# A hybrid four-layer model in fp32 halves: ScalarE, VectorE, GpSimd and the DMA queue ordered by the compiler's other timing model

## The chip, the cores and the metric

The kernel runs on one core of a Trainium2 chip. The metric is the device time in microseconds (us) of one execution. Of the kernel before, three runs are given, with a median of 2611.88 us (2609.99 to 2614.97).

## What is computed

Four layers act on 1040 tokens (16 meta tokens ahead of 1024) of width 1024. Each normalises the running sum `h`, runs one mixer and adds its output to `h`:

```python
for i in range(DEPTH):            # DEPTH = 4; kinds 0, 1, 2, 0
    u = rmsnorm(h, norm_gain[i])
    if kind == 0:   y = attention_branch(u, ...)   # 16 heads, window 128, sinks
    elif kind == 1: y = mlstm_branch(u, ...)       # 8 heads, 128 x 256 state
    else:           y = hgrn2_branch(u, ...)       # 8 heads, 128 x 128 state
    h = h + y
# attention: s = q k^T / 8 in a band; p = exp(s - m) / (sum + exp(sink - m)); o = p v
```

The products are carried in fp32 as sums over a high and a low half of each operand.

## The kernel before

All matmuls work on three column chunks of the tokens (400, 384 and 256 wide). A projection (L254, L299) multiplies weight tiles `wh`, `wl` with the normalised input `uh`, `ul`: three matmuls for each product (high by high, high by low, low by high), eight 128-row pieces deep. The output projections (L337) do the same with `yh`, `yl` and are added to the row `x` by VectorE (L340).

A helper, `split`, makes the halves: a cast on ScalarE (`s.copy`, L187), then a subtraction on VectorE (L188). It serves the weights (128x512, two for each weight tile), the inputs and the outputs alike, so each weight tile costs ScalarE two casts.

The attention layers (the first and the last) run over eight tiles `t` of two heads each. For each group of query blocks and each of the two heads `hh`, a unit is a chain of engines. In `S_step` TensorE makes the scores `pm` (L614, L615), ScalarE copies them into `Sm` (L634), VectorE merges the band (L635) and takes the maximum (L636, L637), ScalarE takes the exponential with its sum (L639), VectorE the reciprocal (L641) and ScalarE scales the row (L643). In `T_step` TensorE then transposes `Sm` (L660) and VectorE masks the result into `Pt` (L663). In `V_step` TensorE multiplies `Pt` with the values (L682) and ScalarE copies the sum out (L685):

```python
for u in range(nu):                                   # end of S_step
    s.activation(Sm[:, u, :P], Sm[:, u, :P], AF.Identity, scale=den[:, u : u + 1])   # L643
...
for u in range(nu):                                   # T_step
    pe.transpose(pt[:, u, :], Sm[:, u, :P], ident)                                   # L660
```

Beside these chains run the projections of the next tile. Their results are handled by the same engines: ScalarE reads `pj` (L519, L520), makes the scales (L536, L538) and splits the queries (casts, L491); VectorE turns them by their positions (L550 to L552). DMAs (L523) rotate the halves of a head. Outer units with a sink use L624, L626 and L628.

The second layer (mLSTM) runs eight heads, 131.8 us apart, each with nine blocks in a chain of its own (L890 to L958) woven into the next head's projections. The third (HGRN2) makes for each region of two blocks the scaled rows `X` by levels (VectorE L1152, L1153, ScalarE L1154, VectorE L1155), multiplies them (L1178), and carries a state `S` (L1255).

What sets the order: the program lists steps with costs in TensorE time, woven by hand. TensorE keeps that order exactly (`tc.manual_schedule` for PE). The other engines are ordered by the compiler's scheduler: it keeps a timeline of its own, and an engine that is free there takes the ready instruction of the highest priority. Priority is the place in the program, and steps wrapped in `hi` (the mixers' chains) count as 40 places earlier. The result is one fixed queue for each engine. In the trace each of these queues is worked off in that order. How long an instruction takes in the scheduler's timeline comes from a timing model, and this is chosen where the context is opened.

## Time and profile before

| | |
|---|---|
| median of the three runs | 2611.88 us |
| the profiled execution's own time | 2610.83 us |
| its span, first to last instruction | 2609.0 us |
| TensorE (PE) busy | 2558.0 us, 98% |
| VectorE (DVE) busy | 1980.3 us, 76% |
| ScalarE (ACT) busy | 1725.9 us, 66% |
| GpSimd (POOL) busy | 154.1 us, 6% |
| mean granted TensorE clock | 0.995 |
| share of the last chain that is TensorE | 81% |

TensorE is the bound: it is idle for 51 us of the span in all, some 15 us of it in the first 60 us. The other engines have idle time, and what they do matters where TensorE waits for it. In the profile PEld is TensorE's weight load, which overlaps its matmuls. In the rows below, a name such as `pt<-ident,Sm` reads: `pt` is written, `ident` and `Sm` are read. A timeline row gives the start, the duration, the engine, the line and the operation, and in brackets how long the engine was idle before it, and who ended that. A waits row gives the total in us, the number of waits and the longest.

### The profile page before, as it was taken

The numbers are of one execution on the slowest core, as the hardware profiler recorded it, in microseconds if no ns is written. First come the engines' busy times: TensorE is split into PE (matmuls) and PEld (weight loads), VectorE is DVE, ScalarE is ACT, GpSimd is POOL, SyncE is SP. The second block draws the span as 40 slices with busy tenths as digits, with TensorE's granted clock in tenths as the row PEclk, the third lists the DMA queues.
The fourth block names the chain that finished last, engine by engine and source line by source line (L and its number), as shares of the span: only waits on it lengthen the run. The fifth ranks groups of instructions, "written<-read, shape, count | busy, mean of one in ns | idle before, by whom it ended". The sixth has DMA issues, their size and how long they took to land.

```text
span 2609.0 us, 56062 instructions
## 1 busy us (share of the span) xinstructions
PE 2558.0 (98%) x21048; PEld 2459.0 (94%) x21048; DVE 1980.3 (76%) x5487; ACT 1725.9 (66%) x4757; POOL 154.1 (6%) x538
## 2 busy tenths in 40 slices
PE   7999999999999999999999999999999999999999
PEld 6899889899999999999999999999999999999999
DVE  6677777986767676767677788978787978677776
ACT  6777776566464646464646857878585867768872
POOL 1100100000000000000000000201001011000000
PEclk9999999999999999999999999999999999999999
DMA  4111111021111111111110101011110111111112
GB/s 136 56 43 50 46 37 47 17 67 58 41 58 41 58 41 58 41 58 41 55 61 34 57 27 42 30 38 34 34 42 26 42 62 45 54 44 47 53 38 82
DMA packets 74048, 126.81 MB, mean 49 GB/s; under 512 B 11552, under 2 KB 25760, under 8 KB 73776
## 3 DMA queue, kind: packets, MB, share of 16 engines
q1 hardware_dynamic: 73776, 123.23, 14.5%
q8 instruction: 165, 2.70, 0.4%
q14 instruction: 107, 0.88, 0.1%
HBM read 108.34 MB, written 4.26 MB: 43 GB/s over the span
## 4 chain that ended last, share of the span: by engine, by line
PE 81%; DVE 10%; ACT 6%; issue 1%; DMA 1%; POOL 0%; SPq 0%; DVEq 0%; ACTq 0%; POOLq 0%
PE pj L254 39%; PE pj L337 16%; PE pj L299 11%; PE po L682 2%; PE pt L660 1%; PE pm L614 1%; PE pm L615 1%; DVE t L407 1%; PE pa L534 1%; DVE ul L188 1%; PE po L918 1%; PE pj L295 1%; PE pm L890 1%; DVE X L1153 1%; DVE X L1155 1%
## 5 line engine op out<-in xcount | busy, mean ns | idle before, releaser
L254 PE MATMUL pj<-uh,wh 128*128 128x384 f32 (+2 forms) x2592 | 870.9, 336 | 3.7 <-ACT uh L187 3.6
L254 PE MATMUL pj<-ul,wh 128*128 128x384 f32 (+2 forms) x2592 | 835.3, 322 | 2.9 <-DVE ul L188 2.8
L254 PE MATMUL pj<-uh,wl 128*128 128x384 f32 (+2 forms) x2592 | 832.9, 321 | 0.1
L254 PEld LDWEIGHTS pj<-uh,wh 128*128 128x128 f32 x2592 | 491.3, 190 | 24.1 <-issue 12.7
L254 PEld LDWEIGHTS pj<-ul,wh 128*128 128x128 f32 x2592 | 491.2, 190 | 8.7 <-DVE ul L188 5.5
L254 PEld LDWEIGHTS pj<-uh,wl 128*128 128x128 f32 x2592 | 490.9, 189 | 0.5 <-DVE wl L188 0.4
L188 DVE TENSOR_TENSOR wl<-wr,wh 128x512 fp32r<-128x512 f32 x336 | 227.9, 687 | 58.1 <-ACT wh L187 55.4
L340 DVE TENSOR_TENSOR x<-x,pj 128x384 f32<-128x384 f32 (+2 forms) x480 | 235.4, 510 | 43.2 <-PE pj L337 41.3
L187 ACT CAST wh<-wr 128x512 fp32r<-128x512 f32 x337 | 203.3, 616 | 83.0 <-PE pj L337 26.8
L299 PE MATMUL pj<-wh,uh 128*128 128x256 f32 x896 | 258.1, 288 | 0.0
L337 PE MATMUL pj<-yh,wh 128*128 128x384 f32 (+2 forms) x768 | 253.0, 329 | 0.0
L299 PE MATMUL pj<-wh,ul 128*128 128x256 f32 x896 | 252.4, 282 | 0.0
L299 PE MATMUL pj<-wl,uh 128*128 128x256 f32 x896 | 252.3, 282 | 0.0
L337 PE MATMUL pj<-yl,wh 128*128 128x384 f32 (+2 forms) x768 | 247.4, 322 | 3.1 <-DVE yl L188 3.1
L337 PE MATMUL pj<-yh,wl 128*128 128x384 f32 (+2 forms) x768 | 246.8, 321 | 0.0
L299 PEld LDWEIGHTS pj<-wh,uh 128*128 128x128 f32 x896 | 169.3, 189 | 1.1 <-issue 0.3
L187 ACT CAST yh<-r 128x400 fp32r<-128x400 f32 (+2 forms) x144 | 68.6, 477 | 153.2 <-PE pj L337 141.7
L299 PEld LDWEIGHTS pj<-wl,uh 128*128 128x128 f32 x896 | 169.3, 189 | 0.5
L299 PEld LDWEIGHTS pj<-wh,ul 128*128 128x128 f32 x896 | 169.3, 189 | 0.0
L428 ACT ACTIVATE t<-t 128x384 f32<-128x384 f32 (+2 forms) x240 | 117.8, 491 | 76.5 <-DVE t L427 74.8
L427 DVE SCALAR_TENSOR_TENSOR t<-pj,t 128x384 f32<-128x384 f32 (+2 forms) x192 | 98.8, 514 | 78.2 <-ACT t L426 75.3
L337 PEld LDWEIGHTS pj<-yl,wh 128*128 128x128 f32 x768 | 144.9, 189 | 5.0 <-DVE yl L188 4.7
(265 smaller groups left out, 5431.4 us busy)
## 6 DMA issues: line engine op xcount, KB each, us to landing
wr<-in_b_win SPq DMA_DIRECT2D x128, 256.0 KB, 2.6
wr<-in_a_win SPq DMA_DIRECT2D x80, 256.0 KB, 2.7
wr<-in_c_win SPq DMA_DIRECT2D x64, 256.0 KB, 2.7
r<-rowsd SPq DMA_DIRECT2D x16, 520.0 KB, 5.4
wr<-in_a_wout SPq DMA_DIRECT2D x32, 256.0 KB, 2.7
wr<-in_b_wout SPq DMA_DIRECT2D x32, 256.0 KB, 2.6
t<-t SPq DMA_DIRECT2D x96, 48.0 KB, 1.9
wr<-in_c_wout SPq DMA_DIRECT2D x16, 256.0 KB, 2.7
```

The source lines that it names most:

```text
L187: s.copy(h, src)
L188: v.tensor_tensor(l, src, h.bitcast(F32), op=ALU.subtract)
L254: pe.matmul(acc[:, :cn], a[:, k, :], b[:, k, c0 : c0 + cn], start=(k == 0 and i == 0), stop=(k == KT - 1 and i == 2))
L295: pe.matmul(acc[:48, :256], um[:, k, :], m[:, kk, :], start=(k == 0 and m is wh), stop=(k == KT - 1 and m is wl))
L299: pe.matmul(acc[:cn, :256], a[:, k, c0 : c0 + cn], m[:, kk, :], start=(k == 0 and i == 0), stop=(k == KT - 1 and i == 2))
L337: pe.matmul(acc[:, :cn], a[:, k, mc], b, start=(k == 0 and i == 0), stop=(k == 1 and i == 2))
L340: v.tensor_tensor(x[:, m, c0 : c0 + cn], x[:, m, c0 : c0 + cn], acc[:, :cn], op=ALU.add)
L407: v.scalar_tensor_tensor(u, x[:, k, cs], ngain[:, self.i, k : k + 1], self.acc[n], op0=ALU.mult, op1=ALU.mult)
L427: v.scalar_tensor_tensor(a[:, :cn], z, 0.0, a[:, :cn], op0=ALU.min, op1=ALU.subtract)
L428: s.activation(a[:, :cn], a[:, :cn], AF.Exp)
L534: pe.matmul(st[:, 2 * k : 2 * k + 2], sq[:, z : z + P], R["masks"][:, 0:P:64], start=True, stop=True)
L682: pe.matmul(po[64 * hh : 64 * hh + 64, q0 - c0 : q0 - c0 + nq], V[kb][:kn, vc : vc + 64], ws[hh]["Pt"][:kn, u, ki, :nq], start=(ki == 0), ...
```

## The change

One argument is added where the context is opened: the scheduler takes the durations and delays of its timeline from the compiler's more detailed timing model.

```diff
-    with tile.TileContext(nc) as tc:
+    with tile.TileContext(nc, schedule_with_timeline_sim=True) as tc:
         hybrid_kernel(tc, ins, out)
```

The instructions are the same. TensorE's queue is the same, row for row. The queues of ScalarE, VectorE, GpSimd and the DMA queue hold the same work in another order. Three places follow.

The first is ScalarE in the first attention layer, between two score copies and the scaling of the row `Sm209` (`wh307` is a weight tile, `t212` and `t197` are query tiles of the projections, `Sm218` is the row of the other head). Before:

```order
L634 COPY Sm209_1226<-pm208_1225 128x2x128
L187 CAST wh307_1670<-wr309_1672 128x512
L639 ACTIVATE Sm209_1226,s211_1228<-Sm209_1226,s210_1227,s164_1013 128x129 x2
L634 COPY Sm218_1269<-pm217_1268 128x2x128
L685 COPY r145_930<-po204_1196 128x384
L519 ACTIVATE t212_1255<-pj205_1205,cons32_224 128x256
L643 ACTIVATE Sm209_1226<-Sm209_1226,s211_1228 128x128 x2
```

Now the same stretch, up to the same row:

```order
L187 CAST wh307_1670<-wr310_1676 128x512
L519 ACTIVATE t212_1255<-pj205_1205,cons32_224 128x256
L520 ACTIVATE t213_1256<-pj205_1205 128x256
L634 COPY Sm218_1269<-pm217_1268 128x2x128
L536 ACTIVATE s222_1287<-pa221_1286,eps_79 128x6
L685 COPY r145_930<-po204_1196 128x384
L538 ACTIVATE s222_1287<-s222_1287 128x6 x2
L491 CAST qs248_1401<-t197_1173 64x384
L491 CAST qs249_1404<-t197_1173 64x384
L639 ACTIVATE Sm209_1226,s211_1228<-Sm209_1226,s210_1227,s164_1013 128x129 x2
L639 ACTIVATE Sm218_1269,s220_1271<-Sm218_1269,s219_1270,s164_1013 128x129
L643 ACTIVATE Sm209_1226<-Sm209_1226,s211_1228 128x128 x2
```

The second weight cast, L520, L536, the two L538, the two L491 and one L639 of the other head stood behind the L643 of `Sm209` and now stand ahead of it.

The second is ScalarE in the last attention layer, at the scaling of `Sm5826` (`wh5902` is a weight tile, `t5829` and `t5811` are query tiles, `Sm5838` belongs to the next unit). Before:

```order
L639 ACTIVATE Sm5820_33373,s5822_33375<-Sm5820_33373,s5821_33374,s5716_32810 128x129 x2
L685 COPY r5772_33131<-po5810_33331 128x384
L643 ACTIVATE Sm5820_33373<-Sm5820_33373,s5822_33375 128x128 x2
L639 ACTIVATE Sm5826_33407,s5828_33409<-Sm5826_33407,s5827_33408,s5716_32810 128x129 x2
L519 ACTIVATE t5829_33430<-pj5816_33361,cons5192_29975 128x256
L643 ACTIVATE Sm5826_33407<-Sm5826_33407,s5828_33409 128x128 x2
```

Now:

```order
L187 CAST wh5902_33786<-wr5905_33792 128x512
L519 ACTIVATE t5829_33430<-pj5816_33361,cons5192_29975 128x256
L520 ACTIVATE t5830_33431<-pj5816_33361 128x256
L536 ACTIVATE s5833_33440<-pa5832_33439,eps_79 128x6
L685 COPY r5772_33131<-po5810_33331 128x384
L643 ACTIVATE Sm5820_33373<-Sm5820_33373,s5822_33375 128x128 x2
L639 ACTIVATE Sm5826_33407,s5828_33409<-Sm5826_33407,s5827_33408,s5716_32810 128x129 x2
L538 ACTIVATE s5833_33440<-s5833_33440 128x6 x2
L491 CAST qs5857_33548<-t5811_33346 64x384
L491 CAST qs5858_33551<-t5811_33346 64x384
L626 ACTIVATE Sm5838_33471,s5840_33473<-Sm5838_33471,s5839_33472 128x145
L643 ACTIVATE Sm5826_33407<-Sm5826_33407,s5828_33409 128x128 x2
```

Both weight casts (the other one stands one row ahead of this piece), L520, L536, the two L538, the two L491 and one L626 came ahead of the L643 of `Sm5826`.

The third is VectorE in the third layer, at the scaled row `X3862` of one region (`X3883` is of the next; the rows with `r3816`, `r3817` and `t3843` belong to the next head's decay). Before:

```order
L1152 TENSOR_TENSOR X3862_21184<-r3733_20207,r3734_20208 128x64x2
L1105 SCALAR_TENSOR_TENSOR r3816_20881<-ones_76,t3843_21058 128x128 x3
L1152 TENSOR_TENSOR X3863_21189<-r3733_20207,r3734_20208 128x128
L1107 SCALAR_TENSOR_TENSOR r3817_20882<-r3817_20882,lb3720_20132,r3816_20881 128x384
L1145 TENSOR_TENSOR X3864_21194<-r3733_20207,r3734_20208 128x256
L1153 TENSOR_TENSOR X3863_21189<-r3733_20207 128x128
L1153 TENSOR_TENSOR X3862_21184<-r3733_20207 128x64x2
L1096 SCALAR_TENSOR_TENSOR t3856_21137<-pj3844_21073,t3855_21136 128x256
L1214 TENSOR_TENSOR X3880_21315<-X3880_21315,Q3783_20640 128x256
L1155 TENSOR_TENSOR X3863_21189<-X3863_21189,Q3783_20640 128x128
L1155 TENSOR_TENSOR X3862_21184<-X3862_21184,Q3783_20640 128x64x2
```

Now:

```order
L1153 TENSOR_TENSOR X3862_21184<-r3733_20207 128x64x2
L1152 TENSOR_TENSOR X3863_21189<-r3733_20207,r3734_20208 128x128
L1153 TENSOR_TENSOR X3863_21189<-r3733_20207 128x128
L1145 TENSOR_TENSOR X3864_21194<-r3733_20207,r3734_20208 128x256
L1155 TENSOR_TENSOR X3859_21163<-X3859_21163,Q3783_20640 128x8x16
L1152 TENSOR_TENSOR X3883_21324<-r3733_20207,r3734_20208 128x2x64
L1153 TENSOR_TENSOR X3883_21324<-r3733_20207 128x2x64
L1102 SCALAR_TENSOR_TENSOR t3819_20884<-t3819_20884,lb3719_20131,t3818_20883 128x400
L1214 TENSOR_TENSOR X3880_21315<-X3880_21315,Q3783_20640 128x256
L1155 TENSOR_TENSOR X3860_21168<-X3860_21168,Q3783_20640 128x16x8
L1155 TENSOR_TENSOR X3861_21173<-X3861_21173,Q3783_20640 128x32x4
L1155 TENSOR_TENSOR X3862_21184<-X3862_21184,Q3783_20640 128x64x2
```

The scans L1105 and the rows L1107 and L1096 of the next head, which stood ahead of the L1155 of `X3862`, stand behind it now.

On the DMA queue, at about a dozen places of the two attention layers a weight load (L232) now stands ahead of the DMAs that rotate a query tile (L523), where it stood behind them. On GpSimd the small copies of the 16 meta tokens (`um`, L412) are grouped in another way.

## Prediction

> **What bounds the kernel now.** I read the page first, then the busy times by stage, then TensorE's waits, and last the timeline at single places. The page says that TensorE is busy for nearly the whole span:

> ```profile
> span 2609.0 us, 56062 instructions
> PE 2558.0 (98%) x21048; PEld 2459.0 (94%) x21048; DVE 1980.3 (76%) x5487; ACT 1725.9 (66%) x4757; POOL 154.1 (6%) x538
> ```

> So a gain can at most be the 51 us in which TensorE is idle, while a loss has no such limit. The busy times by stage (from, to, then the busy time of PE, PEld, DVE, ACT and POOL, then the granted clock, the DMA share and GB/s) say where the idle time lies:

> ```profile
> 0.00:60.00 60.00, 45.04 (x259) 37.93 (x260) 42.02 (x89) 40.05 (x86) 12.88 (x27) 0.97 0.44 141
> 60.00:440.00 380.00, 368.82 (x2697) 339.28 (x2696) 276.94 (x774) 284.99 (x890) 30.99 (x102) 0.99 0.16 49
> 620.00:1540.00 920.00, 919.24 (x6276) 908.97 (x6275) 650.88 (x1730) 539.33 (x1359) 7.32 (x108) 1.00 0.15 50
> 1540.00:2130.00 590.00, 578.08 (x7225) 554.27 (x7224) 502.00 (x1610) 435.88 (x1229) 61.85 (x146) 1.00 0.12 38
> 2200.00:2560.00 360.00, 357.48 (x2704) 337.00 (x2703) 263.54 (x706) 275.78 (x840) 26.11 (x83) 1.00 0.16 49
> ```

> The start loses 15.0 us, the first attention layer (60 to 440) 11.2, the mLSTM heads (620 to 1540) 0.8, the third layer 11.9, the last attention layer (2200 to 2560) 2.5. In both attention layers ScalarE is the busiest engine beside TensorE, 75% and 77%, and 59% among the mLSTM heads. Who ends TensorE's waits (total, times, longest):

> ```profile
> PE pt L660 <- ACT Sm L643: 10.9, 12, 1.9
> PE pa L381 <- DVE t L373: 9.0, 3, 7.8
> PE po L1245 <- DVE S L1255: 5.6, 12, 1.4
> PE pj L337 <- DVE yl L188: 3.1, 6, 0.7
> PE pm L1178 <- DVE X L1155: 2.5, 1, 2.5
> ```

> The longest total is the transpose L660 that waits for ScalarE's scaling L643. Cut to 60 to 440, the same view has ten of these twelve waits; cut to 2200 to 2560, the other two:

> ```profile
> PE pt L660 <- ACT Sm L643: 9.7, 10, 1.9
> ```
> ```profile
> PE pt L660 <- ACT Sm L643: 1.2, 2, 0.8
> ```

> So in the first attention layer the scaling has no time to spare at most of its heavy units, and in the last it has little. Whatever stands between the exponential and the scaling in ScalarE's queue is paid by TensorE.

> **The first attention layer.** TensorE does the same work, so the sum is made of its waits alone. The first place shown of the order is the scaling of `Sm209`. ScalarE there (start, duration, line, idle time before it):

> ```profile
> 104.51 0.62 ACT L187 CAST wh<-wr 128x512 fp32r<-128x512 f32 x1 [0.88 <-PE pj L254]
> ...
> 107.24 0.69 ACT L643 ACTIVATE Sm<-Sm,s 128x128 f32<-128x128 f32 x2
> 107.82 0.38 ACT L520 ACTIVATE t<-pj 128x256 f32<-128x256 f32 x1
> 108.08 0.27 ACT L536 ACTIVATE s<-pa,eps 128x6 f32<-128x6 f32 x1
> 108.23 0.52 ACT L491 CAST qs<-t 64x384 fp32r<-64x384 f32 x1
> 108.64 0.32 ACT L538 ACTIVATE s<-s 128x6 f32<-128x6 f32 x2
> 108.96 0.51 ACT L491 CAST qs<-t 64x384 fp32r<-64x384 f32 x1
> 109.50 0.49 ACT L639 ACTIVATE Sm<-Sm,s,s 128x129 f32<-128x129 f32 x1
> 109.90 0.19 ACT L639 ACTIVATION_READ_ACCUMULATOR Sm<-Sm,s,s 128x1 f32 x1
> ...
> 111.42 0.60 ACT L187 CAST wh<-wr 128x512 fp32r<-128x512 f32 x1
> ```

> and TensorE's transposes of that row:

> ```profile
> 107.69 0.62 PE L660 MATMUL pt<-ident,Sm 128*128 128x128 f32 x2
> ```

> The two transposes start as the two scalings end: no slack. Now the rows from 107.82 to 109.90 and the cast from 111.42 stand ahead: 0.38 + 0.27 + 0.52 + 0.32 + 0.51 + 0.49 + 0.19 + 0.60 = 3.28 us. Between 104.51 and 107.24 ScalarE is never idle, so nothing hides them, and what comes ahead (the L491, which wait for VectorE's turned queries) cannot run in the 0.88 us of idle time ahead of 104.51. TensorE waits some 3.2 us more. What is late next is TensorE's next scores and so the next unit's chain, all of it shifted alike; the other head's scaling, behind it, has then the less ahead of it.

> The order repeats this at nine more places of this layer, with the first half of a tile's heavy units: casts of the next weights and L519, L520, L536, L538 and L491 of the next tile come between. Counted in the same way with these rows they put 3.3 to 4.9 us ahead of the scaling, of which 0 to 2.1 us is slack, and net they stand near the worked place. I take ten times 3.0 = 30 us. Four lighter places (0.5 to 1.4 us) add 3. Bounds: with a cover of 2 us at each, ten times 1.2 = 12; with 4.5 at each, 45.

> **The last attention layer.** The second place is the scaling of `Sm5826`. TensorE's transposes and ScalarE's scaling:

> ```profile
> 2432.91 0.38 PE L660 MATMUL pt<-ident,Sm 128*128 128x128 f32 x2
> ```
> ```profile
> 2431.66 0.69 ACT L643 ACTIVATE Sm<-Sm,s 128x128 f32<-128x128 f32 x2
> 2432.25 0.37 ACT L520 ACTIVATE t<-pj 128x256 f32<-128x256 f32 x1
> 2432.51 0.25 ACT L536 ACTIVATE s<-pa,eps 128x6 f32<-128x6 f32 x1
> ```

> Both weight casts (0.62 and 0.60 by the rows above), L520 (0.37), L536 (0.25), two L538 (0.32), two L491 (1.03) and an L626 (half a microsecond, my estimate from the L639 beside it) come ahead: 3.7 us. The scaling ends at 2432.35 and the transpose starts at 2432.91, so 0.6 us is slack and 3.1 is paid. This is among the dearest of fifteen such places here. At the others the order puts 1.5 to 4.2 us ahead, and the slack is larger, as the 1.2 us of waits says. I take half of the worked price at each: 15 x 1.5 = 22 us; bounds 0.5 and 3.1 at each, 8 and 46.

> **The clock.** TensorE's granted clock falls to half after some of its idle spells. Two idle spells end at 261.04 (1.87 us, TensorE waits for an L643) and 1638.56 (2.46 us):

> ```profile
> 256.00:261.00 5.00, 3.17 (x25) 2.53 (x24) 3.97 (x12) 4.94 (x15) 0.00 (x0) 1.00 0.00 0
> 261.00:264.40 3.40, 3.36 (x13) 3.05 (x14) 2.70 (x8) 3.01 (x11) 0.18 (x1) 0.50 0.00 0
> 111.30:114.70 3.40, 3.40 (x31) 2.95 (x32) 2.53 (x8) 2.08 (x9) 0.18 (x1) 1.00 0.02 5
> 1640.00:1643.40 3.40, 3.40 (x13) 3.38 (x12) 2.74 (x11) 1.09 (x4) 0.00 (x0) 0.50 0.02 5
> ```

> Both are followed by 3.4 us at 0.50, which is 1.7 us of work lost. A wait of 1.83 us that ended at 111.28 was followed by 1.00. So about half of the spells near 1.9 us cost it, and I take it for those near 3 us that they mostly do: ten of the first layer and four of the last, 14 x 1.7 x 0.6 = 14 us; bounds 0 and 25 x 1.7 = 42. [...]

> **The other stages.** In the third place of the order the next head's L1105 scans, L1107 and L1096 no longer stand ahead of the L1155 for which TensorE waits longest in this layer:

> ```profile
> 1634.82 1.04 DVE L1105 TENSOR_TENSOR_SCAN r<-ones,t 128x128 f32<-128x128 f32 x3
> 1635.97 0.61 DVE L1107 SCALAR_TENSOR_TENSOR r<-r,lb,r 128x384 f32<-128x384 f32 x1
> 1637.24 0.41 DVE L1096 SCALAR_TENSOR_TENSOR t<-pj,t 128x256 f32<-128x256 f32 x1
> ```

> That is 2.1 us less ahead, and 1.7 us of half clock behind it. VectorE's rows for `yl` (3.1 us of waits in all) come earlier as well; some L1255 come earlier, some later by 1.2 us. I take -6 us for all of this, between -14 (all waits for `X`, `S` and `yl`, 11.2, and the clock) and +6. Among the mLSTM heads TensorE loses 0.8 us in 920, and ScalarE has two fifths of its time free: nothing, by my choice; its bound is a rival below. At the start and at the head of the last layer three input rows of L407 stand ahead of an L188 for which TensorE waits: 3 us, between 0 and 6.

> On the DMA queue a weight load that moves ahead of the rotation of a query tile may hold it back while it waits for its buffer. The turned tile is used one tile later, some 20 us, which hides it: 0. If that cover were gone, each costs up to one landing, 2.7 us, at about a dozen places:

> ```profile
> wr<-in_a_win SPq DMA_DIRECT2D x80, 256.0 KB, 2.7
> ```

> GpSimd's regrouped copies are needed once in a layer, and only by the projection of the values: 0.

> **The sum.** 30 + 3 + 22 + 14 - 6 + 3 = 66 us. A part will be taken up, since a wait gives ScalarE and VectorE time to catch up for the place behind it, and I take a sixth off the waits: 56 us. The profiled execution took 2610.83 us (its span and 1.8 us around it), 1.05 below the median 2611.88. Against the median I forecast **2668 us**.

> **The rivals.**

> *The clock does not fall* (chance 0.18). If only spells longer than any of these bring half the clock, the 14 us go: 2654 us. For it speaks the spell at 111.28; against it those at 261.04 and 1638.56. [...]

> *The other chains are late too* (0.22). The weight casts and the next head's activations also move between the steps of the mLSTM chains, and between those of the third layer's state updates. If each of the 72 mLSTM blocks waits as the `yl` waits do now (0.7 us at the longest), that is 50 us on top: 2718 us. It decides as soon as a chain's slack is below what is put ahead of it. Against it: 0.8 us of idle time in 920 says that slack is there.

> *It is taken up* (0.07). ScalarE is idle for a quarter of the attention layers. If what comes ahead runs in this time, nothing is left but -6 + 3: 2609 to 2615 us, within 0.2% of the median, about what a measurement of this kernel can tell from no change. The row at 104.51, with only 0.88 us idle in front of the worked place, speaks against it.

> *Faster* (0.07). VectorE's results come earlier at the waits named, and the scaling is late only on paper because its inputs come earlier as well. Then the waits for `X`, `S` and `yl` (11.2 us) and a half-clock spell or two (3.4) go: 2597 us. It decides if the scalings L643 start no later than now; the ten waits without slack speak against it.

> **How the numbers follow.** The forecast has 0.46. The low end of its terms (12 + 0 + 8 + 0 - 14 + 0, next to nothing) meets the third rival, the high end (45 + 6 + 46 + 42 + 6 + 6 = 151) passes the second. Leaving out the two lowest cases and the last few of the highest, the range is 2620 to 2745. The chances are 0.07 faster by over 0.2%, 0.07 within it, and 0.86 slower (0.46 + 0.18 + 0.22).

> **What would show it.** In the profile after, the waits of L660 for L643 (PE, now 10.9 us) should be 40 to 80 us, and the two attention stages should hold most of the growth: some 35 to 45 us between 60 and 440, and 20 to 25 us in the last layer, clock spells included. The mLSTM heads should still be about 131.8 us apart; if each is 5 us longer, the second rival holds. If the stage from 60 to 440 is not at least 10 us longer, the argument fails, since ten scalings without slack then found cover that I do not see. The granted clock should fall below 0.99.

## The result and the profile after

| | before | after |
|---|---|---|
| median (4 runs each, lowest to highest) | 2610.93 us (2608.14 to 2614.97) | 2741.10 us (2737.23 to 2747.37) |
| span of the profiled execution | 2609.0 us | 2739.0 us |
| mean granted clock | 0.995 | 0.981 |

After takes 1.0502 times as long as before (95% interval 1.0488 to 1.0516), 130 us more. The forecast was 2668, 56 us more: the time lies in the range that was given (2620 to 2745), near its upper end, and the loss is more than twice the forecast one. The page of after begins like this:

```profile
span 2739.0 us, 56180 instructions
PE 2610.4 (95%) x21048; PEld 2491.0 (91%) x21048; DVE 1981.7 (72%) x5487; ACT 1729.9 (63%) x4757; POOL 149.3 (5%) x538
```

VectorE and ScalarE are busy for as long as before (1980.3 and 1725.9 us there), as the same work should take. TensorE is busy 52 us longer and idle 78 us longer. The stages, cut at the same matmuls as in the prediction (from and to, length, busy times, clock):

```profile
0.00:63.30 63.30, 45.75 (x259) 39.25 (x260) 41.70 (x89) 40.07 (x86) 14.22 (x27) 0.95 0.40 134
63.30:494.70 431.40, 391.65 (x2697) 358.73 (x2696) 280.01 (x774) 287.93 (x890) 31.80 (x102) 0.93 0.14 43
678.90:1621.00 942.10, 929.17 (x6276) 909.74 (x6275) 652.80 (x1732) 540.63 (x1360) 7.39 (x108) 1.00 0.15 48
1621.00:2222.40 601.40, 582.18 (x7226) 558.04 (x7225) 497.59 (x1609) 434.11 (x1228) 51.58 (x147) 0.99 0.12 38
2296.90:2689.90 393.00, 369.96 (x2704) 343.00 (x2703) 262.79 (x705) 277.17 (x840) 29.55 (x83) 0.98 0.15 45
```

Against before, the first attention layer (second row) is 51.4 us longer (380.0 to 431.4), the mLSTM heads 22.1 (920.0 to 942.1), the third layer 11.4 (590.0 to 601.4), the last attention layer 33.0 (360.0 to 393.0). The start takes 3.3, and the pieces between these stages take 8.8 (4.2 ahead of the heads, 4.5 ahead of the last attention layer, 0.1 at the end). The clock in both traces is 1.0 or 0.5 at any time, so the time at half clock is twice what is missing from the mean: 2 x (1 - 0.995) x 2609 = 26 us before, 2 x (1 - 0.981) x 2739 = 104 us after. Who ends TensorE's waits in after (total, times, longest):

```profile
PE pt L660 <- ACT Sm L643: 56.6, 38, 5.3
PE po L1245 <- DVE S L1255: 13.4, 14, 2.8
PE pa L381 <- DVE t L373: 10.2, 5, 7.6
PE po L920 <- DVE wl L188: 4.4, 7, 0.7
PE po L918 <- ACT wd L187: 3.7, 7, 0.5
```

The wait for the scaling has grown from 10.9 us to 56.6. Waits that before hardly had, L920 and L918 of the mLSTM heads, are new, and the wait for the state (L1255) has more than doubled. At the first worked place, the scaling of `Sm209`, ScalarE and TensorE stand in after like this (start, duration, operation, idle time before it):

```profile
113.18 0.31 ACT L538 ACTIVATE s<-s 128x6 f32<-128x6 f32 x2
113.39 1.03 ACT L491 CAST qs<-t 64x384 fp32r<-64x384 f32 x2
114.44 0.50 ACT L639 ACTIVATE Sm<-Sm,s,s 128x129 f32<-128x129 f32 x1
...
116.07 0.49 ACT L639 ACTIVATE Sm<-Sm,s,s 128x129 f32<-128x129 f32 x1 [0.56 <-DVE s L641]
116.47 0.19 ACT L639 ACTIVATION_READ_ACCUMULATOR Sm<-Sm,s,s 128x1 f32 x1
116.56 0.68 ACT L643 ACTIVATE Sm<-Sm,s 128x128 f32<-128x128 f32 x2
```
```profile
117.00 0.63 PE L660 MATMUL pt<-ident,Sm 128*128 128x128 f32 x2 [2.95 <-ACT Sm L643]
```

The steps that the prediction named stand ahead of L643, the transposes start as the scalings end, and TensorE waits 2.95 us there (forecast some 3.2).

### The profile page after: what moved, and what is told of

Same layout as the page of the kernel before. It is cut to its first block, busy times and chain, and to the rows that moved or that the text cites. A ratio compares the mean times of both kernels' runs of the same rounds, so it can differ in the third digit from the quotient of the medians.

```text
span 2739.0 us, 56180 instructions
## 1 busy us (share of the span) xinstructions
PE 2610.4 (95%) x21048; PEld 2491.0 (91%) x21048; DVE 1981.7 (72%) x5487; ACT 1729.9 (63%) x4757; POOL 149.3 (5%) x538
## 4 chain that ended last, share of the span: by engine, by line
PE 68%; DVE 15%; ACT 10%; DMA 3%; issue 2%; SPq 1%; POOL 0%; DVEq 0%; ACTq 0%; POOLq 0%
PE pj L254 31%; PE pj L337 15%; PE pj L299 10%; DVE wl L188 2%; PE po L682 2%; ACT wh L187 1%; ACT Sm L639 1%; PE pt L660 1%; DVE t L407 1%; DVE r L852 1%; PE pm L614 1%; PE pm L615 1%; DVE ul L188 1%; DMA t<-t 1%; DMA wr<-in_a_wout 1%
## 5 line engine op out<-in xcount | busy, mean ns | idle before, releaser
L254 PE MATMUL pj<-uh,wh 128*128 128x384 f32 (+2 forms) x2592 | 878.4, 339 | 3.6 <-ACT uh L187 3.6
L254 PE MATMUL pj<-ul,wh 128*128 128x384 f32 (+2 forms) x2592 | 842.1, 325 | 6.9 <-DVE ul L188 6.7
L254 PE MATMUL pj<-uh,wl 128*128 128x384 f32 (+2 forms) x2592 | 838.9, 324 | 0.1
L254 PEld LDWEIGHTS pj<-uh,wh 128*128 128x128 f32 x2592 | 497.6, 192 | 23.7 <-issue 13.3
L254 PEld LDWEIGHTS pj<-ul,wh 128*128 128x128 f32 x2592 | 496.4, 191 | 13.5 <-DVE ul L188 10.4
L254 PEld LDWEIGHTS pj<-uh,wl 128*128 128x128 f32 x2592 | 495.9, 191 | 0.5 <-DVE wl L188 0.4
L188 DVE TENSOR_TENSOR wl<-wr,wh 128x512 fp32r<-128x512 f32 x336 | 226.7, 689 | 62.9 <-ACT wh L187 60.0
L187 ACT CAST wh<-wr 128x512 fp32r<-128x512 f32 x337 | 196.6, 617 | 101.1 <-PE pj L337 31.5
L337 PE MATMUL pj<-yh,wh 128*128 128x384 f32 (+2 forms) x768 | 253.9, 331 | 0.0
L337 PE MATMUL pj<-yl,wh 128*128 128x384 f32 (+2 forms) x768 | 247.8, 323 | 2.2 <-DVE yl L188 2.2
L337 PE MATMUL pj<-yh,wl 128*128 128x384 f32 (+2 forms) x768 | 247.4, 322 | 0.0
L187 ACT CAST yh<-r 128x400 fp32r<-128x400 f32 (+2 forms) x144 | 67.4, 478 | 132.2 <-PE pj L337 127.4
L337 PEld LDWEIGHTS pj<-yl,wh 128*128 128x128 f32 x768 | 145.5, 189 | 3.6 <-DVE yl L188 3.3
## 6 DMA issues: line engine op xcount, KB each, us to landing
wr<-in_b_win SPq DMA_DIRECT2D x128, 256.0 KB, 2.8
wr<-in_a_win SPq DMA_DIRECT2D x80, 256.0 KB, 2.8
wr<-in_c_win SPq DMA_DIRECT2D x64, 256.0 KB, 2.6
wr<-in_a_wout SPq DMA_DIRECT2D x32, 256.0 KB, 3.0
wr<-in_b_wout SPq DMA_DIRECT2D x32, 256.0 KB, 3.0
wr<-in_c_wout SPq DMA_DIRECT2D x16, 256.0 KB, 2.7
```

Source lines behind the costliest of these rows:

```text
L187: s.copy(h, src)
L188: v.tensor_tensor(l, src, h.bitcast(F32), op=ALU.subtract)
L254: pe.matmul(acc[:, :cn], a[:, k, :], b[:, k, c0 : c0 + cn], start=(k == 0 and i == 0), stop=(k == KT - 1 and i == 2))
L337: pe.matmul(acc[:, :cn], a[:, k, mc], b, start=(k == 0 and i == 0), stop=(k == 1 and i == 2))
```

## Experiments

Most of them pin one engine's queue to a written order, on top of either kernel. The numbers are those of the instructions, which are the same in both kernels:

```
+def pin(tc, numbers):
+    at = {i.name: i for i in tc.nc.cur_bb.bb.instructions}
+    names = [f"I-{n}" for n in numbers if f"I-{n}" in at]
+    for a, b in zip(names, names[1:]):
+        tc.add_manual_dep(at[b], a, mybir.DependencyInfo(mybir.DependencyClass.NoSync, mybir.DependencyReason.DATA), reason="pin")
```

The theory at the outset (A) was the prediction's own: ScalarE's queue in the attention layers makes most of the loss. The rivals were VectorE's queue (B) and a loss spread over all engines and stages (C).

**One queue at a time.** First ScalarE's queue as before, under the detailed model:

```
     with tile.TileContext(nc, schedule_with_timeline_sim=True) as tc:
         hybrid_kernel(tc, ins, out)
+        pin(tc, ACT_ORDER_OF_BEFORE)
```

> The detailed model places all engines but ScalarE, whose queue is pinned, instruction by instruction, to the one of before. Theory A (ScalarE's queue puts casts and the next tile's steps ahead of the scaling L643 in the attention layers, and the half-clock spells follow from these waits): nearly all of the 130 us comes back, 2615 to 2650 us; the waits of L660 for L643 fall from 56.6 to under 20 us and the stage from 60 to 440 of before is under 10 us longer than in before. Rival B (VectorE's order does it): over 2700 us. Rival C (spread over all engines and stages): about 2680 us, with the mLSTM heads as long as in after (942 us).

Measured: 2724.8 us, 1.0435 of before (1.0419 to 1.0450). Only 16 of the 130 us came back and the waits of L660 for L643 are still 37.4 us, so theory A falls in the form in which it was written. The same with VectorE's queue (`pin(tc, DVE_ORDER_OF_BEFORE)`):

> The detailed model places all engines but VectorE, whose queue is pinned to the one of before. Theory A (ScalarE's queue): VectorE's order matters little, 2690 us or more, and the waits of L660 for L643 stay at 40 us or more. Rival B (VectorE's order): 2650 us or less. Rival C (spread over all engines): about 2680 us.

Measured: 2727.7 us (1.0448; 1.0433 to 1.0464). Rival B falls too, though the waits of L660 for L643 fall to 34.2 us. The totals hide part of it. In the two attention layers, which are 84 us longer in after than in before, ScalarE's queue as before leaves 58 of them (34 and 24) and VectorE's 43 (27 and 16), while the heads and the third layer come out longer than in after (943.9 and 609.2 us with ScalarE's, 955.7 and 620.1 with VectorE's, against 942.1 and 601.4). And the reverse of the first, ScalarE's queue of after pinned under the default model (`TileContext(nc)` and `pin(tc, ACT_ORDER_OF_AFTER)`):

> The reverse of the first: the default model places all engines but ScalarE, whose queue is pinned to the one of after. Theory A (ScalarE's queue alone makes the loss): 2690 us or more, with waits of L660 for L643 of 40 us or more. Rival B (VectorE's order is needed for it): 2640 us or less.

Measured: 2766.3 us (1.0597; 1.0579 to 1.0615), waits of L660 for L643 61.3 us, so more than after itself. What undid the first run in the attention layers is seen in ScalarE's own waits in the first of them, with ScalarE's queue as before (top) and in before (below):

```profile
ACT Sm L639 <- DVE s L637: 30.9, 28, 5.7
```
```profile
ACT Sm L639 <- DVE s L637: 12.0, 14, 2.0
```

The scores' chain goes back and forth between the two engines: L634 on ScalarE, L635 to L637 on VectorE, L639 on ScalarE, L641 on VectorE, L643 on ScalarE. The model places anew whatever is not pinned, and then the other half of the chain is late: ScalarE's exponentials L639 wait 30.9 us instead of 12.0 (22.4 in after). So next both were pinned, and only GpSimd and the DMA queue were left to the detailed model:

> The detailed model places only GpSimd and the DMA queue; ScalarE's and VectorE's queues are both pinned to those of before. Theory A, mended after the first two runs (the attention chain runs through both engines, and either order alone makes it late; together they hold the whole loss): 2605 to 2625 us, waits of L660 for L643 of 10 to 14 us. Rival D (the DMA queue's or GpSimd's order has a part in it): 2640 us or more.

Measured: 2615.7 us, 1.0019 of before (1.0007 to 1.0032), waits of L660 for L643 10.8 us. ScalarE's and VectorE's queues together hold 125 of the 130 us. GpSimd's queue comes out as in before here, so the 5 us that are left (2 to 8 by the interval) are the DMA queue's. At the start the loads of two weights now stand behind the masks and the rotation tables, and the first 60.0 us of before take 63.6.

**Where it lies.** The attention layers keep the order of before on all four queues, the rest is left to the detailed model (`pin` with those instructions alone):

> The detailed model, but the instructions of the two attention layers keep among themselves the order of before on all four queues; the mLSTM heads and the third layer are left to the detailed model. Theory A (the attention layers hold 84 of the 130 us): 2645 to 2665 us, with the two attention stages as long as in before (380 and 360 us) and the mLSTM heads still near 942 us. Rival C (the loss is the same everywhere once anything is placed by the detailed model, with the stages only shifting it among themselves): over 2700 us.

Measured: 2648.2 us (1.0142; 1.0127 to 1.0158). The stages:

```profile
58.20:437.00 378.80, 367.73 (x2698) 338.09 (x2697) 276.56 (x774) 285.52 (x890) 30.99 (x102) 1.00 0.16 49
620.40:1562.80 942.40, 929.46 (x6276) 909.96 (x6275) 652.88 (x1732) 542.02 (x1360) 7.36 (x108) 1.00 0.15 49
2234.70:2595.10 360.40, 357.25 (x2703) 336.60 (x2702) 263.85 (x706) 275.70 (x840) 25.85 (x83) 1.00 0.16 49
```

The attention layers are as short as in before and the heads as long as in after. 93 of the 130 us hang on the order inside the attention layers, 37 on that of the rest. Now the mLSTM layer alone as before:

> The detailed model, but the instructions of the mLSTM layer keep among themselves the order of before on all four queues; the other layers are left to the detailed model. If the order inside the mLSTM heads makes their loss: the stage of the heads is 920 to 923 us long again (942.1 in after) and the time 2714 to 2724 us. If what was late came from outside of the layer (the input rows, the DMA queue's state, the next layer's casts): 2735 us or more, and heads as long as in after.

Measured: 2719.4 us (1.0406; 1.0391 to 1.0422), heads 920.2 us. Their 22 us come from the order inside the heads.

**The prediction's step by itself.** Everything as before, but ahead of 86 scalings L643 of the attention layers stand the ScalarE instructions that after puts there:

```
     with tile.TileContext(nc) as tc:
         hybrid_kernel(tc, ins, out)
+        pin(tc, ACT_ORDER_OF_BEFORE_WITH_289_MOVED_AHEAD)
+        pin(tc, DVE_ORDER_OF_BEFORE)
+        pin(tc, POOL_ORDER_OF_BEFORE)
+        pin(tc, SP_ORDER_OF_BEFORE)
```

> The queues of before, except that ahead of 86 scalings L643 of both attention layers the ScalarE instructions are put that stand there in after (289 casts, next-tile steps and others; groups that cannot run in this order are left where they were). VectorE, GpSimd and the DMA queue keep the order of before. If the sum of the prediction holds for ScalarE by itself (33 us in the first attention layer, 22 in the last, some clock): 2655 to 2685 us, waits of L660 for L643 of 45 to 70 us. If VectorE's order is needed for most of it: 2615 to 2640 us. If what is put ahead also brings its own waits for VectorE, which the sum left out: over 2690 us.

Measured: 2695.8 us (1.0332; 1.0317 to 1.0346), 86 us more than before. TensorE's waits and the three large stages:

```profile
PE pt L660 <- ACT Sm L643: 62.8, 41, 5.7
```
```profile
58.50:501.50 443.00, 393.96 (x2696) 357.71 (x2696) 275.83 (x774) 287.83 (x890) 30.88 (x102) 0.93 0.14 42
681.10:1602.40 921.30, 919.96 (x6277) 908.93 (x6276) 650.17 (x1729) 538.82 (x1359) 7.32 (x109) 1.00 0.15 50
2263.70:2646.40 382.70, 364.61 (x2703) 338.32 (x2702) 263.03 (x706) 277.73 (x840) 24.77 (x83) 1.00 0.15 46
```

The attention layers grow by 63 and 23 us, 86 together (in after 84, as 51 and 33), the heads hardly. So theory A holds for the attention layers, as the prediction meant it: what stands ahead of L643 in ScalarE's queue is enough for a loss as large as theirs. It is not needed, since with ScalarE's queue as before these layers still lose 58 us. The waits, 62.8 us, 52 more than in before, are within what the sum expected of them (55 more). The time is above it, and above the 2690 from which the waits that the moved steps bring were to be blamed. They are not the reason, as the waits came out no longer than forecast: what lies between 52 and 86 us is not idle time, and a good part of it is the clock, 0.93 in the first of these rows. The same for VectorE, its steps alone moved ahead, was not tried.

**The clock.** The same queues as in after, but TensorE gets something to do while it waits for L643 in 14 places (a helper that is called ahead of L660; it transposes the identity into a part of `pt` that nothing reads):

```
-                    pe.transpose(pt[:, u, :], Sm[:, u, :P], ident)
+                    keep_busy(nc, "T", pt[:, 3, :], ident); pe.transpose(pt[:, u, :], Sm[:, u, :P], ident)
```

> The four queues as in after, but TensorE transposes the identity into an unused part of the same PSUM bank, 141 times in all, during the 14 waits of 1.8 us and more of L660 for L643, so that it is hardly idle there (work added, none taken away). If idle time is what brings the half clock and the half clock costs what the sum of the stages says: of 107.7 us at half clock some 60 go, half of which is time, 2708 to 2722 us. If ScalarE and VectorE set the pace of these stretches, so that a faster TensorE only waits longer: 2733 to 2745 us, at a higher clock.

Measured: 2728.9 us (1.0449; 1.0435 to 1.0463), 12 us less than after. The two attention layers:

```profile
63.10:482.40 419.30, 389.49 (x2812) 356.97 (x2812) 279.71 (x774) 287.24 (x890) 31.98 (x102) 0.98 0.15 44
2288.80:2676.60 387.80, 367.83 (x2729) 341.06 (x2728) 261.69 (x703) 276.47 (x839) 30.39 (x83) 1.00 0.15 45
```

In this execution of 2725.7 us the clock rises from 0.981 to 0.991, which is 2 x (1 - 0.991) x 2725.7 = 49 us at half clock instead of 104 (the other three executions had 0.986 to 0.989). So it is idle time that brings the half clock, as expected. But neither number came: the two layers are 12.1 and 5.2 us shorter, 17 us for some 59 us at half clock (0.07 of twice 431 and 0.02 of twice 393, less 0.02 of twice 419), three tenths of a microsecond for each and not a half. The 43 executions of before that were timed beside these runs give a price without any added work, as they differ in the clock: twelve at 0.995 took 2612.3 us on average and three at 0.998 took 2606.2, which is 6.1 us for 2 x 0.003 x 2610 = 15.7 at half clock, or 0.39. (One of the 43 does not fit: 0.956, but 2605.7 us.) Some of what is gained turns into new waits: behind the place shown above the second transposes now wait, which they did not do in after.

```profile
119.75 0.62 PE L660 MATMUL pt<-ident,Sm 128*128 128x128 f32 x2 [0.62 <-ACT Sm L643]
```

**A version slightly faster than both.** Before has six half-clock spells of its own within its span. TensorE is kept busy in the same way at three of its places:

```
+FILL = {("first", 0): 4, ("T", 52): 6, ("X", 125): 8}
...
-                        pe.matmul(pf[g0 : g0 + w, b, lv - 2, :w], X[:, P * b + g0 : P * b + g0 + w],
+                        keep_busy(nc, "X", W["pf"][:, 384:512], ident); pe.matmul(pf[g0 : g0 + w, b, lv - 2, :w], X[:, P * b + g0 : P * b + g0 + w],
```

> The four queues as in before, with 18 transposes of the identity at three places of before at which a wait of 1.3 to 2.5 us is followed by half the clock (the first L651, one L660, one L1178 of the first head of the third layer). If idle time brings the half clock: three spells of 3.4 us go (25.6 us at half clock before, some 15 then), 2604 to 2607 us. If it comes for another reason, or the dummy work delays what follows: 2610 to 2614 us.

Measured: 2606.8 us, 0.9986 of before (0.9977 to 0.9994). Its profiled execution has a clock of 0.997, which is 2 x (1 - 0.997) x 2608 = 16 us at half clock where before has 26. With eight places and more transposes at each:

```
+FILL = {("first", 0): 8, ("X", 125): 17, ("C", 0): 8, ("T", 2): 10, ("T", 12): 12, ("T", 52): 12, ("T", 82): 8, ("T", 96): 7}
```

> The queues of before, with 84 transposes of the identity at eight places of before at which TensorE waits 1.2 to 2.5 us (five L660, the first L651, one L1178, the first L1250), sized to leave about a quarter of a microsecond. If idle time brings the half clock: only the spells that come from the short waits at 517 and 2196 are left, under 12 us at half clock (25.6 in before), and 2600 to 2606 us. If the dummy work delays what follows: 2608 to 2615 us.

Measured: 2606.4 us, 0.9988 (0.9979 to 0.9997), a clock of 0.999 in the profiled execution, which is 2 x (1 - 0.999) x 2605 = 5 us at half clock.

Three to four microseconds are what was gained at these places. The interval leaves out 1, though the gain is under 0.2%, and the time is just above what was expected. The three executions of before that had a clock of 0.998 took 2606.0 to 2606.3 us without any added work: the two versions make regular what 3 of the 43 executions of before had.

## Why the prediction was right in its direction and wrong in its size

**Attention, waits: right.** 30 + 3 us were forecast for the first layer and 22 for the last, on top of the 9.7 and 1.2 of before. TensorE's waits for L643 in these layers in after:

```profile
PE pt L660 <- ACT Sm L643: 36.5, 18, 5.3
```
```profile
PE pt L660 <- ACT Sm L643: 20.1, 20, 3.2
```

That is 27 and 19 us more, 46 in all, and 46 is what the 55 come to when a sixth is taken off. That it comes so close holds some luck: with ScalarE's steps alone moved, which is what the sum counted, the same waits grew by 37 and 15 us. Of the worked places the first waited 2.95 us (3.2 forecast). The sum of 3.28 there counts some time twice, since ScalarE's rows overlap (the one at 107.82 is 0.38 long and the next starts 0.26 behind it); from the first start to the last end they take 2.27, and with the cast some 2.8. The second place waited 1.28 us (3.1 forecast), less than the half that the prediction took for its fifteen places, while twenty of them waited:

```profile
2548.79 0.62 PE L660 MATMUL pt<-ident,Sm 128*128 128x128 f32 x2 [1.28 <-ACT Sm L643]
```

**The clock: the right mechanism, too small.** The term was 14 us, from 14 spells with 1.7 us each at a chance of 0.6. The attention layers of after hold 0.07 x 431.4 x 2 + 0.02 x 393.0 x 2 = 76 us at half clock, some 68 more than before, which is twenty windows of 3.41 us. The term reckoned 14 x 0.6 = 8.4 of them. At the three tenths of a microsecond that keeping TensorE busy gave back for each us at half clock, or the 0.39 of the executions of before, the 68 us are 20 to 27 (estimates from those runs), and at the half that the prediction took, 34. The step that failed is "about half of the spells near 1.9 us cost it", taken as a chance: in these traces the half clock goes by how much of a wait falls into one window of 3.41 us (counted in the last section). The windows in before around the two waits that the prediction compared, that of 1.83 us that ended at 111.28 and that of 1.87 that ended at 261.04:

```profile
107.41:110.82 3.41, 2.03 (x12) 1.42 (x10) 2.92 (x9) 3.37 (x14) 0.19 (x1) 1.00 0.35 115
110.82:114.24 3.42, 2.96 (x29) 2.69 (x30) 2.44 (x9) 2.10 (x10) 0.18 (x1) 1.00 0.02 5
257.60:261.01 3.41, 1.57 (x12) 1.06 (x8) 2.41 (x9) 3.40 (x11) 0.00 (x0) 1.00 0.00 0
261.01:264.43 3.42, 3.39 (x13) 3.08 (x14) 2.69 (x8) 3.03 (x11) 0.18 (x1) 0.50 0.00 0
```

The half-clock spells of before, and those of after, start on one grid of 3.41 us each. The wait at 111.28 is cut by an edge of it, 1.38 us of idle time on one side and 0.46 on the other, and nothing follows. The one at 261.04 lies in one window, 1.84 us idle, and the next window has 0.50. In after the waits of the first attention layer are 1.9 to 5.3 us long at eleven of its units, and behind nine of the eleven, or within them, the clock is half (the two without it, of 1.86 and 2.08 us, leave at most 1.2 us idle in one window). Seven of the ten spells of this layer run over two windows:

```profile
114.25:117.67 3.42, 0.67 (x4) 0.52 (x5) 2.82 (x8) 2.83 (x12) 0.00 (x0) 1.00 0.50 169
117.67:121.08 3.41, 3.41 (x16) 3.21 (x15) 2.82 (x9) 2.14 (x9) 0.38 (x2) 0.50 0.03 8
121.08:124.49 3.41, 3.41 (x24) 3.16 (x22) 0.70 (x5) 0.67 (x4) 0.00 (x0) 0.50 0.00 0
```

The rival "the clock does not fall" is refuted by the mean clock of 0.981 (0.995 in before).

The stage rows split the 84 us of the attention layers: 49 more are idle time and 35 busy time. Of the busy part the clock has 20 to 27 us; what the rest is was not worked out.

**The heads and the third layer: the step that failed most.** "Among the mLSTM heads TensorE loses 0.8 us in 920 ...: nothing, by my choice", and "-6 us for all of this" for the third layer and the chains around. Measured: 22.1 us in the heads, 11.4 in the third layer and 4.2 in the piece ahead of the heads, 38 instead of -6. That is 44 of the 74 us by which the forecast fell short (130 less 56); the attention layers have some 25 more, of which the clock is 6 to 13. The rival "the other chains are late too" came nearest, with 2718 us at a chance of 0.22. It said that it decides as soon as a chain's slack is below what is put ahead of it, and the prediction held the 0.8 us against it. But idle time of nearly nothing says that slack is not negative; it does not say how much there is. The place to read it is from the end of the producer to the start of its consumer. In the first heads of before, VectorE's product `E` (L913), ScalarE's cast of it to `wd` and TensorE's L918 that uses `wd`:

```profile
708.76 0.28 DVE L913 TENSOR_TENSOR E<-E,pm 128x128 f32<-128x128 f32 x1
```
```profile
709.07 0.30 ACT L187 CAST wd<-E 128x128 fp32r<-128x128 f32 x1 [0.71 <-DVE E L913]
```
```profile
711.07 0.28 PE L918 MATMUL po<-v,wd 128*128 128x258 f32 x1
```

The cast ends at 709.37, so the slack is 1.7 us. After changes both queues. On VectorE two rows L852 of the next projection, which stood behind this L913, now stand ahead of it (the second is shown), and on ScalarE two steps of that projection stand ahead of the cast:

```profile
770.67 0.63 DVE L852 SCALAR_TENSOR_TENSOR r<-t,bcols,r 128x400 f32<-128x400 f32 x1
771.22 0.28 DVE L913 TENSOR_TENSOR E<-E,pm 128x128 f32<-128x128 f32 x1
```
```profile
771.34 0.54 ACT L424 ACTIVATE t<-r 128x400 f32<-128x400 f32 x1 [1.27 <-DVE r L852]
771.78 0.46 ACT L846 COPY t<-pj 128x384 f32<-128x384 f32 x1
772.14 0.30 ACT L187 CAST wd<-E 128x128 fp32r<-128x128 f32 x1
```
```profile
772.59 0.36 PE L918 MATMUL po<-v,wd 128*128 128x258 f32 x1 [0.53 <-ACT wd L187]
```

TensorE's last matmul ahead of L918 starts at 710.96 in before and at 771.77 in after, 60.81 us later. Against this, `E` (709.04, now 771.50) is 1.65 us late, which is nearly the whole slack. The two L852, 0.55 us each from start to start, make 1.1 of it; the rest came from ahead of them on VectorE. The two ScalarE steps then put the cast 0.64 us behind `E`, where it followed at once, and TensorE waits. The 1.27 us that ScalarE waits at L424 add nothing, since `E` was not there either. Some eight microseconds later in the same head L920 waits 0.63 us for the low half `wl` of such an `E`. The cast is long done by then, and VectorE's subtraction stands behind rows of the projection:

```profile
779.17 0.30 ACT L187 CAST wd<-E 128x128 fp32r<-128x128 f32 x1
```
```profile
780.20 0.48 DVE L852 SCALAR_TENSOR_TENSOR r<-t,bcols,r 128x256 f32<-128x256 f32 x1
780.60 0.28 DVE L188 TENSOR_TENSOR wl<-E,wd 128x128 fp32r<-128x128 f32 x1
```

These two waits return in each of the next heads, with smaller ones at L1001. A head comes out some 3 us longer (22.1 by the seven that the stage holds). That is the rival's mechanism, at 22 us and not 50, as it happens at a few places of a head and not at every block, and at these two places VectorE's order has the larger share. What each engine's order costs over all the heads was not settled: with ScalarE's queue as before they were 23.9 us longer than in before, with VectorE's 35.7.

In the third layer the wait of 2.5 us that the prediction reckoned away, L1178 for `X`, is gone. But the waits for the state grew from 5.6 to 13.4 us, and the longest shows the same pattern. TensorE has `pa` ready at 1722.03; VectorE's state update L1255 that reads it now stands behind other rows, among them five L1155 of the region, while in before it started as soon as `pa` was there (last row):

```profile
1721.64 0.39 PE L1250 MATMUL pa<-v,kT 128*128 128x128 f32 x2
1725.08 0.57 PE L1245 MATMUL po<-X,S 128*128 128x128 f32 x2 [2.83 <-DVE S L1255]
```
```profile
1723.34 1.09 DVE L1155 TENSOR_TENSOR X<-X,Q 128x128 f32<-128x128 f32 x5
...
1724.68 0.34 DVE L1255 SCALAR_TENSOR_TENSOR S<-S,s,pa 128x128 f32<-128x128 f32 x1
```
```profile
1643.83 0.35 DVE L1255 SCALAR_TENSOR_TENSOR S<-S,s,pa 128x128 f32<-128x128 f32 x1 [1.09 <-PE pa L1250]
```

The prediction saw that some of these updates come later, by 1.2 us, and set the earlier ones against them; no run took the third layer's order by itself.

**The rest.** The start and the head of the last layer were forecast at 3 us together and took 3.3 and 4.5. The DMA queue was forecast at 0 and has the 5 us of the run that left it to the detailed model. Three tell-tales failed: the heads 131.8 us apart, 35 to 45 us more in the first attention layer (51.4) and 20 to 25 more in the last (33.0). The waits of L660 (40 to 80 us), the clock below 0.99 and most of the growth in the two attention layers (84 of 130 us) came as said.

## What to carry to other kernels

Before a change of the order is called free in a stage, read the slack of each of its chains, from the end of a producer to the start of its consumer, and follow the chain back through every engine that it passes, adding up what the new order puts ahead on each; an engine that is never idle tells nothing of that. Where a chain passes to and fro between two engines, pinning one of them does not cure it, since the other's queue can make it late alone; and read such a run stage by stage, as its total can hide what came back. A wait on TensorE can cost more than its length: count the clock behind it (here 1.84 us of idle time in one window were followed by 3.41 us at 0.50).

## What the runs showed of the hardware that was not expected

In the head above a break cost TensorE more than its row shows as idle. A matmul's row there is 0.28 us long while the next one starts 0.12 us behind it. So L918, which starts 0.70 us later behind the matmul before it than in before, shows 0.53 as idle, and the missing 0.16 is counted as busy. Of the 22 us by which the heads grew, the rows show 12 as idle and 10 as busy, at the full clock. So the busy time of this stage grew from 919.2 to 929.2 us though TensorE does nothing more in it, 6276 matmuls in both.
